# V's quads among the gate quads, and V's stores one to a product, in a hybrid decoder block on one Trainium2 core

## The chip, the cores and the metric

The kernel runs on one core of one Trainium2 chip. The core has five engines that run side by side: TensorE (PE: matmuls, with its weight loads listed as PEld), VectorE (DVE), ScalarE (ACT), GpSimd (POOL) and SyncE (SP), which here only issues DMAs. Each engine works through its own queue in order and waits on semaphores. The metric is the device time of one execution in microseconds (us). The kernel before the change takes 2109.99 us, the median of three runs (2107.88 to 2110.27).

## What is computed

One decoder block, for 2048 tokens of width 1024, all in float32. Cut to what matters here:

```python
proj = x @ w_in[l] + b_in[l]
q, k, v, g_attn, u_lru, g_lru, gate_logits = jnp.split(proj, SPLIT_POINTS, axis=-1)
q, k = rope(q), rope(k)                      # 3 groups of 8 heads of 64
for g, (window, dilation) in enumerate(((128, 1), (512, 4), (2048, 16))):
    o_g, lse_g = dilated_band_attention(q[:, :, g], k[:, :, g], v[:, :, g], window, dilation)
attn = sum over g of softmax(lse)_g * o_g
y_a = (attn * jax.nn.silu(g_attn)) @ w_attn_proj[l]
u = causal_depthwise_conv(u_lru, conv_w[l], conv_b[l])
y_b = (rg_lru(u, ...) * jax.nn.silu(g_lru)) @ w_lru_proj[l]
merged = sigmoid(gA) * y_a + sigmoid(gB) * y_b
x = layer_norm(ALPHA * x + merged @ w_out[l] + b_out[l])
```

The columns of proj form 72 tiles of 128: 12 each for q, k and v, 4 for the attention gate (ga), 8 each for u, its gate, and the two merge gates.

## The kernel before, in words

The kernel has three stages. The first, the projection, is the one that the change touches; it ends near 1454 us. Attention follows until about 1653 us, and then the merge and the output. Later stages read what the projection stored in device memory (names that end in _scr).

*The projection.* The 2048 tokens are worked in two halves of 1024. In each half the 72 column tiles go in 36 pairs, called quads here (two column tiles by two token chunks of 512), which gives 72 quads, numbered 0 to 71. Nearly all quads use Strassen's scheme in Winograd's form: 7 products in place of 8. There are 505 products in all. One product (function product, L602) is 12 matmuls of 128x128 by 128x512 (L620): over four row blocks, each of three terms, h times the input's high part, h times its low part, and l times the high part. h and l are the high and the low part of a weight block (fp32r), or of a sum of blocks (S). ACT makes h (L269), and l is made by DVE (L227, called at L275 in prep_w). In the first half the l's are also stored (wl_scr, L282); in the second they are loaded from there (L287).

*Order of the quads.* The table seq (L539 to L546) sets it: 2 merge-gate quads, then groups of "qk" quads (a k tile and a q tile) and "ug" quads (u and its gate), with places between them that take the next entry of the list light. In light stand first the six V quads, then two ga quads, then six merge-gate (mg) quads. So in each half the V quads stand at the places 4, 7, 9, 12, 15 and 17; ga at 20 and 23; mg at 25, 28, 31, 33 to 35. In the second half 36 is added to each.

*What follows a product.* The main loop (L941) goes through the products by number. For each it records the product's matmuls, then the steps that are due (weight loads load_w, L234; preparation of h and l three or four products ahead of their use), then run_chains (L187), then evacuate (L632), which adds the product into results. A finished result of 128x512 starts a chain, a generator that goes one step further when its Ask allows: a lag in products, a number of vacant slots, and a budget of time on the engines. The order in which this Python code records instructions is the order of every engine's queue.

- qk_chain (L299): four loads of a copy of the result with its 32-row blocks swapped (sw, L307, issued by SP), then at least two products later the rotation (y times cos, sw times sin, their sum, all at L227 on DVE, in the second half partly on POOL), then stores to k_scr, qh_scr and ql_scr.
- v_chain (L351): DVE transposes the result in 32x32 blocks (L355, vs<-y); then four stores to v_scr (L362), each 64 KB in pieces of 128 bytes, two after one product and two after the next at the earliest. A V quad has four results, so 16 stores; all twelve V quads have 192.
- mg_chain and silu_chain: the gates, on ACT mostly, with one store of 256 KB for each result.
- lru (L439): convolution and recurrence, on ACT and DVE.

*Slots.* Results, weights and helper tiles take 128x512 slots from one pool of NS = 32 (take, L133; the one that has been vacant longest comes first). give_sent (L150) gives a slot back two products after its last store was issued; whoever takes it next waits until that store has landed.

SP's queue therefore holds, in the order of the recording, weight loads, sw loads, stores of k, q, V, gates and l's, and in the second half the loads of l.

Of the kernel before, what the change touches and what calls it, by code (L numbers as in the profile page):

```python
# [26 lines left out]
FT_Q, FT_K, FT_V = 0, 12, 24  # L27
FT_GA, FT_U, FT_GL, FT_MA, FT_MB = 36, 40, 48, 56, 64
# [3 lines left out]
def hybrid_block_kernel(ctx: ExitStack, tc: tile.TileContext, a: dict, out: bass.AP):  # L32
    nc = tc.nc
    sp, act, dve, pool, pe = nc.sync, nc.scalar, nc.vector, nc.gpsimd, nc.tensor

    def flat(t):
        return t.bitcast(F32)
# [54 lines left out]
    late, pe_late = [], []  # L92

    def later(lag, fn):
        late.append((now["n"] + lag, fn))
# [4 lines left out]
    def run(queue):  # L100
        due = [x for x in queue if x[0] <= now["n"]]
        queue[:] = [x for x in queue if x[0] > now["n"]]
        for _, fn in due:
            fn()
# [19 lines left out]
    stA = ctx.enter_context(ExitStack())  # L124
    sl_p = stA.enter_context(tc.tile_pool(name="sl_p", bufs=1))
    ps = stA.enter_context(tc.tile_pool(name="ps", bufs=2, space=PSUM))
    NS, NL = 32, 4
    LATE = [7, 8, 9, 10, 11, 12, 13]
    TRACE = False
    vacant = list(range(NS))  # L130
# [2 lines left out]
    def take(name, dt=F32R):  # L133
        if not vacant:
            raise RuntimeError(f"no slot at {now['n']}: {[x[1].name if hasattr(x[1],'name') else x[1] for x in home.values()]} chains {len(chains)}")
        i = vacant[0]
        if name[0] == "y" and now["n"] >= base[NQ - 1]:
            i = next((x for x in LATE if x in vacant), i)
            if i in LATE:
                LATE.remove(i)  # L140
        vacant.remove(i)
        t = sl_p.tile([P, CH], dt, tag=f"s{i}", name=name)
        home[id(t)] = (i, t)
        return t

    def give(*ts):
        for t in ts:
            vacant.append(home.pop(id(t))[0])

    def give_sent(*ts):  # L150

        for t in ts:
            later(2, lambda t=t: give(t))
# [16 lines left out]
    chains = []  # L170
# [6 lines left out]
    def spend(**eng):  # L177
        for k, v in eng.items():
            if k == "DVE" and now["n"] < base[len(seq)] - 6:
                v *= ALONE  # L180
            left[k] = left.get(k, 0.0) - v
# [44 lines left out]
    def tt(eng, out, in0, in1, op):  # L226
        eng.tensor_tensor(out=out, in0=in0, in1=in1, op=op)  # L227
# [123 lines left out]
    def v_chain(vt, sgn, f, c):  # L351
        g, hp = divmod(f - FT_V, 4)
        yield Ask(need=1, DVE=.72)
        vs = take(f"vs{f}_{c}", F32)
        dve.transpose(vs, flat(vt))  # L355
        give(vt)
        dst = v_scr[g][hp // 2][c * CH:(c + 1) * CH].rearrange("(b i) f -> i b f", i=32)
        for a in range(4):
            if a % 2 == 0:
                yield Ask()  # L360
            f0 = (hp % 2) * P + 32 * a
            sp.dma_start(dst[:, :, f0:f0 + 32], vs[32 * a:32 * a + 32].rearrange("p (b f) -> p b f", f=32))  # L362
        give_sent(vs)


    def store_chain(t, dst):
        yield Ask()
        sp.dma_start(dst, t)
        give_sent(t)
# [49 lines left out]
    begun, gated, done = ({i: 0 for i in range(8)} for _ in range(3))  # L419
# [117 lines left out]

    qk = [("qk", FT_K + u, FT_Q + u) for u in range(12)]
    mg = [("mg", FT_MA + i, FT_MB + i) for i in range(8)]  # L539
    light = [("v", FT_V + 2 * j, FT_V + 2 * j + 1) for j in range(6)]  # L540
    light += [("ga", FT_GA + 2 * j, FT_GA + 2 * j + 1) for j in range(2)] + mg[2:]
    ug = [("ug", FT_GL + i, FT_U + i) for i in range(8)]
    seq = mg[:2]
    for i in range(8):
# [22 lines left out]
    def result(s, fi, c, bank, u):  # L567

        kind = plan[s][4]
        f = plan[s][1][fi][0]  # L570
        sgn = -1.0 if fi else 1.0
        nm = f"{f}_{c}"
        if u is None:
            y = take("y" + nm, F32)
            spend(ACT=.7)
            start_chain(mg_chain(y, 1.0, f, c, bank))
            return
        if kind in ("qk", "v"):
            y = take("y" + nm)
            total(flat(y), bank, u, f, sgn, True)  # L580
            start_chain(qk_chain(y, f, c) if kind == "qk" else v_chain(y, sgn, f, c))
        elif kind == "mg":
            y = take("y" + nm, F32)
            total(y, bank, u, f, sgn, False)
            start_chain(mg_chain(y, sgn, f, c))
        elif kind == "ga" or not fi:
            y = take("y" + nm, F32)
            total(y, bank, u, f, sgn, False)
            start_chain(silu_chain(y, sgn, f, c))
        else:  # L590
            i = f - FT_U
            if c == 1 and i in put_off:
                y = take("y" + nm, F32)
                total(y, bank, u, f, sgn, True)
                act.activation(ubs[:, i, 2, 0:3], y[:, CH - 3:CH], AF.Copy)
                start_chain(store_chain(y, u_scr[i]))
                return
            ub = ub_free.pop(0)
            total(ub[:, 3:3 + CH], bank, u, f, sgn, True)
            start_chain(lru(i, c, ub), 7 if c % 2 else 0)  # L600
# [31 lines left out]
    def evacuate(s, j):  # L632
        half, _, order, _, _ = plan[s]
        c0, c1 = 2 * half, 2 * half + 1
        if order is None:
            fi, k, c = PLAIN[j]
            if k:
                result(s, fi, c0 + c, Q["b"], None)
            return
        pid = order[j]  # L640
        b = Q[s, "p5"] if order is MID and pid in (5, 3) else Q["b"]
        if pid == 1:
            Q["e"] = take(f"e{s}", F32)
            act.activation(Q["e"], b, AF.Copy)
        elif pid == 2:
            result(s, 0, c0, b, Q["e"])
        elif pid == 6:
            Q["u2"] = take(f"u{s}", F32)
            tt(dve, Q["u2"], Q["e"], b, ALU.subtract)
        elif pid == 7:  # L650
            Q["u3"] = take(f"v{s}", F32)
            tt(dve, Q["u3"], Q["u2"], b, ALU.add)
        elif pid == 5:
            result(s, 1, c1, b, Q["u3"])
            if order is MID:
                Q[s, "u2"] = Q.pop("u2")
            else:
                tt(dve, Q["u2"], Q["u2"], b, ALU.add)
            if "p3" in Q:
                result(s, 0, c1, Q["p3"], Q["u2"])  # L660
                spend(DVE=.9)
        elif pid == 4:
            result(s, 1, c0, b, Q["u3"])
        elif order is MID:
            u2 = Q.pop((s, "u2"))
            result(s, 0, c1, b, u2)
            give(u2)
            return
        elif order.index(5) > j:
            Q["p3"] = take(f"p{s}", F32)  # L670
            act.activation(Q["p3"], b, AF.Copy)
        else:
            result(s, 0, c1, b, Q["u2"])
        last = {"e": (2, 6), "u2": (3, 5), "u3": (4, 5), "p3": (5,)}
        for n, p in last.items():
            if order is MID and n == "u2":
                continue
            if n in Q and pid in p and all(order.index(x) <= j for x in p):
                give(Q.pop(n))
# [119 lines left out]
    def unit(u):  # L799

        return (0, 2, 1)[u % 3], u // 3
# [139 lines left out]
    for T, (s, j) in enumerate(where):  # L941
        now["n"] = T
        for k in ("PE", "ACT", "DVE", "POOL"):
            left[k] = min(left[k], 0.0) + LEN
        if plan[s][2]:
            spend(**COST[plan[s][2][j]])
        product(s, j)
        for fn in events.pop(T, []):
            fn()
        run(late)  # L950
        run_chains()
        if T >= base[NQ - 1]:
            for fn in ((), first[:2], first[2:], (), second[:2], firstv, second[2:], ())[T - base[NQ - 1]]:
                fn()
        evacuate(s, j)
        low = min(low, len(vacant))
        if TRACE:
            print(T, s, j, plan[s][4], len(vacant), len(lo_vacant), len(chains), {k: round(v, 1) for k, v in left.items()})
    n = len(where)
    while chains or late or pe_late:  # L960
        now["n"] = n
        for k in left:
            left[k] = LEN
        run(pe_late)
        run(late)
        run_chains()
        n += 1
        assert n < len(where) + 60, (len(chains), late, pe_late)
# [171 lines left out]
    for i in range(NG):  # L1140
# [10 lines left out]
        light = copied and (unit((i - 2) // 4)[0] == 2 or i % 3 == 1 or i == 2)  # L1151
# [223 lines left out]
    for n in range(32):  # L1375
        c, f = divmod(n, 8)
# [159 lines left out]
    for tt in range(16):  # L1536
        c, b = divmod(tt, 4)
# [68 lines left out]
```

## Time and profile before

| | |
|---|---|
| median of 3 runs | 2109.99 us (2107.88 to 2110.27) |
| the profiled execution's own time | 2113.87 us |
| its span | 2112.2 us |
| PE busy | 2076.5 us (98%) |
| DVE busy | 1672.9 us (79%) |
| ACT busy | 1093.8 us (52%) |
| POOL busy | 472.0 us (22%) |
| SP's DMA queue | 480.63 MB in 349232 packets, 71.3% of 16 engines' span |
| V's stores | 192 of 64 KB, median 3.5 us from issue to landing |
| PE's share of the chain that ended last | 85%, L620 alone 58% |

A row of the profile names a line of the kernel, an engine, an operation and "out<-in" by the program's tile names, and then a count. In a timeline it begins with the start and the length in us, and brackets at its end hold the engine's idle time before it and what ended that. "SPq" is SP's queue at the time that it issues a DMA, which is not the time of the transfer. The profile comes from one execution, the times from others.

### The profile page before, as it was taken

The numbers are of one execution on the slowest core, as the hardware profiler recorded it, in microseconds if no ns is written. First come the engines' busy times: TensorE is split into PE (matmuls) and PEld (weight loads), VectorE is DVE, ScalarE is ACT, GpSimd is POOL, SyncE is SP. The second block draws the span as 40 slices with busy tenths as digits, with TensorE's granted clock in tenths as the row PEclk, the third lists the DMA queues.
The fourth block names the chain that finished last, engine by engine and source line by source line (L and its number), as shares of the span: only waits on it lengthen the run. The fifth ranks groups of instructions, "written<-read, shape, count | busy, mean of one in ns | idle before, by whom it ended". The sixth has DMA issues, their size and how long they took to land.

```text
span 2112.2 us, 35066 instructions
## 1 busy us (share of the span) xinstructions
PE 2076.5 (98%) x11696; PEld 1710.3 (81%) x11696; DVE 1672.9 (79%) x3146; ACT 1093.8 (52%) x2293; POOL 472.0 (22%) x436
## 2 busy tenths in 40 slices
PE   8999899999999999999998999999999999999998
PEld 7888788788888888887887888888888888888887
DVE  8889689788888878887886988976999645576667
ACT  6346246257356566556655775666999411211100
POOL 1111111111111012232221222221424344431120
PEclk9999999999999999999999999999999999999999
DMA  9898998988987967778788888779896798964432
GB/s 276 257 266 229 249 266 238 241 264 256 275 287 237 347 198 208 223 222 222 230 257 237 256 251 261 247 244 342 312 346 221 214 313 275 299 220 156 162 105 70
DMA packets 369590, 516.26 MB, mean 244 GB/s; under 512 B 173057, under 2 KB 178177, under 8 KB 366081
## 3 DMA queue, kind: packets, MB, share of 16 engines
q1 hardware_dynamic: 349232, 480.63, 71.3%
q0 software_dynamic: 12256, 19.42, 5.5%
q10 hardware_dynamic: 7920, 13.97, 1.9%
q8 instruction: 93, 1.52, 0.3%
q14 instruction: 89, 0.72, 0.1%
HBM read 312.95 MB, written 186.25 MB: 236 GB/s over the span
## 4 chain that ended last, share of the span: by engine, by line
PE 85%; ACT 5%; SPq 3%; DMA 3%; DVE 2%; issue 1%; DVEq 0%; ACTq 0%
PE q L620 58%; ACT p L1037 4%; PE yb L1354 3%; PE yb L1355 3%; PE z L1464 3%; PE z L1465 3%; PE yb L1356 3%; PE z L1466 3%; PE o L1078 2%; SPq L362 2%; PE s L1022 1%; PE ya L1432 1%; PE ya L1433 1%; PE ya L1434 1%; PE g L484 1%; PE pt L1048 1%
## 5 line engine op out<-in xcount | busy, mean ns | idle before, releaser
L620 PE MATMUL q<-xT,hS 128*128 128x512 f32 x1680 | 520.6, 391 | 0.0
L620 PE MATMUL q<-xT,l 128*128 128x512 f32 x1120 | 437.1, 390 | 4.0 <-DVE l L227 4.0
L620 PE MATMUL q<-xB,hA 128*128 128x512 f32 x1248 | 393.1, 396 | 11.9 <-ACT xB L215 5.6
L620 PEld LDWEIGHTS q<-xT,hS 128*128 128x128 f32 x1680 | 315.7, 189 | 70.6 <-issue 5.2
L620 PE MATMUL q<-xB,l 128*128 128x512 f32 x904 | 356.3, 394 | 9.0 <-DVE l L227 5.9
L620 PEld LDWEIGHTS q<-xB,hA 128*128 128x128 f32 x1248 | 237.0, 191 | 67.0 <-issue 6.7
L620 PEld LDWEIGHTS q<-xT,l 128*128 128x128 f32 x1120 | 211.1, 188 | 49.1 <-DVE l L227 4.9
L620 PEld LDWEIGHTS q<-xB,l 128*128 128x128 f32 x904 | 172.0, 190 | 47.6 <-DVE l L227 7.6
L269 ACT ACTIVATE hA<-wA 128x512 fp32r<-128x512 f32 x218 | 135.0, 622 | 92.5 <-DMA wA<-in_w_in_dram 26.3
L620 PE MATMUL q<-xT,hA 128*128 128x512 f32 x560 | 174.4, 393 | 0.0
L1037 ACT ACTIVATE p<-p,sta 128x256 f32<-128x256 f32 (+1 forms) x384 | 173.0, 473 | 1.1 <-DVE sta L1029 1.1
L245 POOL DMA_DIRECT2D wS<-in_w_in_dram x70 | 61.8, 955 | 497.7 <-DMA wS<-in_w_in_dram 158.0
L620 PE MATMUL q<-xB,hS 128*128 128x512 f32 x560 | 172.5, 389 | 0.0
L269 ACT ACTIVATE hS<-S 128x512 fp32r<-128x512 f32 x175 | 107.8, 622 | 97.1 <-DVE S L227 23.3
L227 POOL TENSOR_TENSOR S<-S,wA 128x512 f32<-128x512 f32 x35 | 48.7, 1392 | 425.0 <-DVE S L227 209.4
L227 DVE TENSOR_TENSOR y<-y,cos 128x512 f32<-128x512 f32 x96 | 81.1, 849 | 60.8 <-DMA sw<-y 60.6
L620 PEld LDWEIGHTS q<-xT,hA 128*128 128x128 f32 x560 | 105.2, 189 | 23.8 <-issue 2.2
L620 PEld LDWEIGHTS q<-xB,hS 128*128 128x128 f32 x560 | 105.0, 188 | 22.2 <-issue 0.4
L1029 DVE CUSTOM_DVE_ANT_0 p<-s,mask 128x256 f32<-128x256 f32 (+1 forms) x384 | 116.5, 360 | 0.2 <-PE s L1022 0.2
L1465 PE MATMUL z<-wo,mh 128*128 128x512 f32 (+1 forms) x264 | 101.0, 383 | 0.0
L1466 PE MATMUL z<-wo,ml 128*128 128x512 f32 (+1 forms) x264 | 101.0, 383 | 0.0
L1464 PE MATMUL z<-wo,mh 128*128 128x512 f32 (+1 forms) x264 | 101.0, 383 | 0.0
(204 smaller groups left out, 4165.3 us busy)
## 6 DMA issues: line engine op xcount, KB each, us to landing
wA<-in_w_in_dram SPq DMA_DIRECT2D x253, 256.0 KB, 4.7
wl_scr<-l SPq DMA_DIRECT2D x105, 512.0 KB, 4.9
l<-wl_scr SPq DMA_DIRECT2D x105, 512.0 KB, 4.4
sw<-y SPq DMA_DIRECT2D x384, 64.0 KB, 2.8
wS<-in_w_in_dram SPq DMA_DIRECT2D x70, 256.0 KB, 4.1
wS<-in_w_in_dram POOLq DMA_DIRECT2D x70, 256.0 KB, 6.4
v_scr<-vs SPq DMA_DIRECT2D x192, 64.0 KB, 3.5
B<-k_scr SPq DMA_DIRECT2D x24, 512.0 KB, 7.7
```

The source lines that it names most:

```text
L227: eng.tensor_tensor(out=out, in0=in0, in1=in1, op=op)
L245: pool.dma_start(t, w_part(s, x), accum_op=ALU.add)
L269: act.activation(h, r, AF.Copy)
L620: pe.matmul(bank, w[:, ks], x[:, kk, xx], start=(first and i == 0 and not onto), stop=(last and i == 11), skip_group_check=onto)
L1029: dve.tensor_tensor_reduce(out=st["p", i, j][:, h, lo:256], in0=st["s", i, j // 2][h][:, j % 2, lo:256], in1=mask[:, lo:256], scale=1.0, s ...
L1037: act.activation(p, p, AF.Exp, scale=-1.0, bias=s[:, h:h + 1], accum_out=s[:, 2 + h:3 + h])
L1354: pe.matmul(yb, WL[f][:, 0, k], xx[:, 0], start=(k == 0), stop=False)
L1355: pe.matmul(yb, WL[f][:, 0, k], xx[:, 1], start=False, stop=False)
L1356: pe.matmul(yb, WL[f][:, 1, k], xx[:, 0], start=False, stop=(k == 7))
L1464: pe.matmul(z, mh[:, k], w[:, 0, hs], start=(k == 0), stop=False)
L1465: pe.matmul(z, mh[:, k], w[:, 1, hs], start=False, stop=False)
L1466: pe.matmul(z, ml[:, k], w[:, 0, hs], start=False, stop=(k == 7))
```

## The change

Three edits, all in the projection. The list light now alternates V quads with ga and mg quads, so that V stands at the places 4, 9, 15, 20, 25 and 31 of each half, ga at 7 and 12, mg at 17, 23, 28 and 33 to 35; the qk and ug quads stay where they were. v_chain no longer issues its stores: it appends them to a list, v_store, and the main loop issues one at the end of each product's work, or two where the list holds more than six (and goes on after the last product until it is empty). The tile vs is given back after its fourth store, as before. NS is 34 in place of 32. Every engine has as many instructions as before, 192 V stores among them: before they were issued in groups of 2, 4, 6 or 8 after 55 of the products, now in groups of 1 or 2 after 148.

```diff
-    NS, NL = 32, 4
+    NS, NL = 34, 4
...
         vs = take(f"vs{f}_{c}", F32)
         dve.transpose(vs, flat(vt))
         give(vt)
+        yield Ask()
         dst = v_scr[g][hp // 2][c * CH:(c + 1) * CH].rearrange("(b i) f -> i b f", i=32)
         for a in range(4):
-            if a % 2 == 0:
-                yield Ask()
             f0 = (hp % 2) * P + 32 * a
-            sp.dma_start(dst[:, :, f0:f0 + 32], vs[32 * a:32 * a + 32].rearrange("p (b f) -> p b f", f=32))
-        give_sent(vs)
-
+            v_store.append((dst[:, :, f0:f0 + 32], vs[32 * a:32 * a + 32].rearrange("p (b f) -> p b f", f=32), vs if a == 3 else None))
+
+
+    v_store = []
+
+    def store_v():
+        for _ in range(1 + (len(v_store) > 6)):
+            if not v_store:
+                return
+            dst, part, done = v_store.pop(0)
+            sp.dma_start(dst, part)
+            if done is not None:
+                give_sent(done)
...
-    light = [("v", FT_V + 2 * j, FT_V + 2 * j + 1) for j in range(6)]
-    light += [("ga", FT_GA + 2 * j, FT_GA + 2 * j + 1) for j in range(2)] + mg[2:]
+    other = [("ga", FT_GA + 2 * j, FT_GA + 2 * j + 1) for j in range(2)] + mg[2:]
+    light = []
+    for j in range(6):
+        light += [("v", FT_V + 2 * j, FT_V + 2 * j + 1), other.pop(0)]
+    light += other
...
         evacuate(s, j)
+        store_v()
...
-    while chains or late or pe_late:
+    while chains or late or pe_late or v_store:
+        store_v()
```

Two places in SP's queue show what this moves. The first is where the V quad 9 of the first half has its stores, ahead of the sw loads of the qk quad 10. In the names, v_scr<-vs is a V store, sw<-y a load of a swapped copy, wA and wS are weight blocks and wl_scr<-l is a store of low halves. Before:

```order
L362 DMA v_scr_77<-vs_1_2302 32x16x32 x2
L362 DMA v_scr_77<-vs_0_2304 32x16x32 x2
L362 DMA v_scr_77<-vs_0_2332 32x16x32 x2
L362 DMA v_scr_77<-vs_1_2334 32x16x32 x2
L362 DMA v_scr_77<-vs_0_2332 32x16x32 x2
L362 DMA v_scr_77<-vs_1_2334 32x16x32 x2
L307 DMA sw_1_2395<-y_1_2368 32x512 x4
L234 DMA wA_12_2418<-in_w_in_dram 128x512
L282 DMA wl_scr_128<-l_11_2325 128x1024
L307 DMA sw_0_2423<-y_0_2400 32x512 x4
```

Four more V stores stand a little ahead of these twelve, with weight loads between, and a third row of sw loads follows after a weight load and a store. The same place after the change:

```order
L371 DMA v_scr_76<-vs_1_2298 32x16x32 x2
L307 DMA sw_1_2379<-y_1_2354 32x512 x4
L371 DMA v_scr_76<-vs_0_2300 32x16x32 x2
L234 DMA wA_12_2404<-in_w_in_dram 128x512
L282 DMA wl_scr_128<-l_11_2321 128x1024
L307 DMA sw_0_2409<-y_0_2384 32x512 x4
L371 DMA v_scr_76<-vs_0_2300 32x16x32 x2
L234 DMA wA_12_2435<-in_w_in_dram 128x512
L282 DMA wl_scr_127<-l_10_2373 128x512
L307 DMA sw_0_2442<-y_0_2414 32x512 x4
L371 DMA v_scr_76<-vs_0_2324 32x16x32 x2
```

With two stores a little ahead of these rows, four V stores now stand ahead of the first sw loads where sixteen stood, six ahead of the second and eight ahead of the third; the others follow behind.

The second place is the V quad 45 of the second half, ahead of the qk quad 46; l<-wl_scr is a load of low halves. SP's queue before:

```order
L362 DMA v_scr_77<-vs_3_9295 32x16x32 x2
L362 DMA v_scr_77<-vs_2_9297 32x16x32 x2
L362 DMA v_scr_77<-vs_2_9299 32x16x32 x2
L307 DMA sw_2_9341<-y_2_9306 32x512 x4
L287 DMA l_47_9363<-wl_scr_128 128x1024
L234 DMA wA_48_9365<-in_w_in_dram 128x512
L234 DMA wA_48_9367<-in_w_in_dram 128x512
L362 DMA v_scr_77<-vs_3_9295 32x16x32 x2
L362 DMA v_scr_77<-vs_2_9297 32x16x32 x2
L362 DMA v_scr_77<-vs_2_9299 32x16x32 x2
L362 DMA v_scr_77<-vs_3_9339 32x16x32 x2
L307 DMA sw_2_9385<-y_2_9346 32x512 x4
```

Two more weight loads, two V stores and the load l_48 follow these rows. After the change:

```order
L307 DMA sw_2_9331<-y_2_9302 32x512 x4
L371 DMA v_scr_76<-vs_3_9291 32x16x32 x2
L287 DMA l_47_9355<-wl_scr_128 128x1024
L234 DMA wA_48_9357<-in_w_in_dram 128x512
L234 DMA wA_48_9359<-in_w_in_dram 128x512
L307 DMA sw_2_9369<-y_2_9336 32x512 x4
L371 DMA v_scr_76<-vs_3_9291 32x16x32 x2
L234 DMA wA_48_9393<-in_w_in_dram 128x512
L234 DMA wA_48_9395<-in_w_in_dram 128x512
L371 DMA v_scr_76<-vs_2_9293 32x16x32 x4
L287 DMA l_48_9451<-wl_scr_129 128x1024
L307 DMA sw_3_9454<-y_3_9430 32x512 x4
```

Sixteen V stores stood ahead of the load l_48, and now eight do; the first sw loads of these rows, which stood behind six stores, stand ahead of all.

## The prediction

> **What bounds the kernel now.** I read the page first, then the busy time by stretches, the waits of TensorE (PE), and at each place where PE stood still the order of time on PE, VectorE (DVE) and SyncE's queue (SP). The page says that PE is nearly always busy:
>
> ```profile
> span 2112.2 us, 35066 instructions
> PE 2076.5 (98%) x11696; PEld 1710.3 (81%) x11696; DVE 1672.9 (79%) x3146; ACT 1093.8 (52%) x2293; POOL 472.0 (22%) x436
> ```
>
> So only PE's losses can be won. The projection ends near 1454 us; here are its stretches, for PE alone. Columns: from and to, length, PE busy (matmul records), granted clock, DMA share, GB/s.
>
> ```profile
> 30.00:230.00 200.00, 200.00 (x887) 1.00 0.90 255
> 230.00:260.00 30.00, 23.49 (x93) 0.89 0.86 229
> 260.00:400.00 140.00, 140.00 (x622) 1.00 0.91 252
> 400.00:430.00 30.00, 24.79 (x88) 0.83 0.87 250
> 430.00:955.00 525.00, 525.00 (x2331) 1.00 0.82 251
> 955.00:985.00 30.00, 28.20 (x117) 0.94 0.82 220
> 985.00:1120.00 135.00, 135.00 (x603) 1.00 0.82 238
> 1120.00:1150.00 30.00, 24.21 (x93) 0.83 0.79 214
> 1150.00:1440.00 290.00, 290.00 (x1291) 1.00 0.80 251
> 180.00:210.00 30.00, 30.00 (x134) 1.00 0.80 223
> ```
>
> PE is busy without a gap at clock 1.00, except in four stretches of 30 us; an undisturbed one (the last row) holds 134 matmuls. I call them stalls 1 to 4. The rows with which PE starts again (start, length, what, idle time before it and its releaser):
>
> ```profile
> 240.13 0.50 PE L620 MATMUL q<-xT,l 128*128 128x512 f32 x1 [1.90 <-DVE l L227]
> 244.22 0.70 PE L620 MATMUL q<-xB,hA 128*128 128x512 f32 x2 [1.53 <-DVE u L227]
> 247.99 0.79 PE L620 MATMUL q<-xB,l 128*128 128x512 f32 x1 [3.07 <-DVE l L227]
> 405.31 0.50 PE L620 MATMUL q<-xT,l 128*128 128x512 f32 x1 [2.13 <-DVE l L227]
> 409.67 0.70 PE L620 MATMUL q<-xB,hA 128*128 128x512 f32 x2 [0.21 <-DVE u L227]
> 413.24 0.79 PE L620 MATMUL q<-xB,l 128*128 128x512 f32 x1 [2.87 <-DVE l L227]
> 967.72 0.50 PE L620 MATMUL q<-xB,l 128*128 128x512 f32 x1 [1.80 <-DMA l<-wl_scr]
> 1131.62 1.22 PE L620 MATMUL q<-xB,hA 128*128 128x512 f32 x2 [4.56 <-ACT hA L269]
> 1134.08 0.79 PE L620 MATMUL q<-xB,l 128*128 128x512 f32 x1 [1.23 <-DMA l<-wl_scr]
> ```
>
> PE lacks weights: l (the low halves) that DVE has not made, or l and hA that come late by DMA. Behind this stands SP's queue; stall 1, then 2, on SP, with DVE's row between:
>
> ```profile
> 222.44 10.63 SPq L362 DMA_DIRECT2D v_scr<-vs  x12
> 233.17 2.41 SPq L307 DMA_DIRECT2D sw<-y  x4
> ...
> 237.20 0.69 DVE L227 TENSOR_TENSOR y<-y,cos 128x512 f32<-128x512 f32 x1 [12.49 <-DMA sw<-y]
> ...
> 388.15 10.18 SPq L362 DMA_DIRECT2D v_scr<-vs  x12
> ```
>
> Twelve V stores in one run hold SP for 10.63 us (0.89 each). The loads of a rotated copy (sw) stand behind them; DVE, which works in order, idles 12.49 us for sw, and its l's stand behind that wait. In the second half it is the weight loads that stand behind V's stores; stall 3:
>
> ```profile
> 943.12 4.01 SPq L362 DMA_DIRECT2D v_scr<-vs  x6
> 951.28 5.66 SPq L362 DMA_DIRECT2D v_scr<-vs  x8
> 960.86 0.96 SPq L362 DMA_DIRECT2D v_scr<-vs  x2
> 961.92 0.59 SPq L287 DMA_DIRECT2D l<-wl_scr  x1
> ```
>
> All four stalls lie where a V quad stands between two qk quads (sequence numbers 9, 17, 45 and 53).
>
> **What the stalls cost.** Against 134, the four stretches lack 41, 46, 17 and 41 matmuls, 145 in all; at 30/134 = 0.224 us that is 32.5 us. A second way: idle time is 120 - 100.7 = 19.3 us, and clock lost while busy is 23.49 x 0.11 + 24.79 x 0.17 + 28.20 x 0.06 + 24.21 x 0.17 = 12.6 us; together 31.9. I take the mean, 32.2 us. Even the shortest stall lowers the clock; the stretch behind its 1.80 us of idle time:
>
> ```profile
> 968.00:972.00 4.00, 4.00 (x13) 3.08 (x13) 3.97 (x6) 1.26 (x2) 1.89 (x2) 0.62 0.77 287
> ```
>
> So stall 3 costs 17 x 0.224 = 3.8 us, not 1.8. The Trainium skill (TensorE: Matmul & The Clock Gate, Part 1) says that the clock drops after an idle window of about 3.4 us; by that rule stall 3 would cost 1.8 us and the sum would be 30.2. The granted clock of 0.62 disagrees, and I go by it.
>
> **The change, part by part.** *Stores in a list.* Each of the 192 stores is still issued by SP, so nothing is removed; they move. At quad 9, 16 stores stood ahead of the first group of sw loads, and now 4 do; ahead of the third group 16, and now 8, two at the end of each of four products. At stall 1's price the first group comes 12 x 0.89 = 10.7 us earlier, the third 8 x 0.89 = 7.1. PE's idle time there was 1.90 by the first wait and 1.90 + 1.53 + 3.07 = 6.50 up to the third, so both are covered, the third by only 0.6 us. A store alone may be cheaper:
>
> ```profile
> L362 SPq DMA_DIRECT2D v_scr<-vs x192: 318/506/3482, 104.3 to 1127.6; - x192
> DMA to landing us min/median/max: 1.9/3.5/6.6
> ...
> 291.41 2.27 SPq L362 DMA_DIRECT2D v_scr<-vs  x2
> 293.79 3.55 SPq L307 DMA_DIRECT2D sw<-y  x4
> 270.00:300.00 30.00, 30.00 (x134) 24.84 (x133) 23.76 (x38) 14.73 (x23) 6.94 (x9) 1.00 0.92 233
> ```
>
> At the median of 0.506 us the eight that stay take 4.0 us and the cover is 3.7; at 1.14, as the pair at 291.41 that stood just ahead of sw loads, they take 9.1 against 14.2 before, and 6.5 - 5.1 = 1.4 us of stall would stay. I take the nearest, the run of stall 1: no stall. At stall 3's place (quad 45) the sixteen stores took 4.01 + 5.66 + 0.96 = 10.63 us ahead of the l load; eight now stand ahead, which is 5.3 us earlier against 1.80 of idle time.
>
> *The order of quads.* Places 17 and 53 hold a gate quad now, so stalls 2 and 4 lose all their V stores. V between two qk quads remains at 9 and 45 and is new at 25 and 61. At 25 six stores stand ahead of the third sw group, fewer than at 9; 61 resembles 45. Gate quads move up behind ug quads at 7, 12, 43 and 48. Before, a ga quad stood behind a ug quad at 20, 23, 56 and 59, and a gate quad between two qk quads at 25 and 61, all inside stretches without a gap (430 to 955, 1150 to 1440). Cost nothing; if ACT's longer silu chains collided at the early places, I bound it by one stall 3, 3.8 us.
>
> *Slots.* V's tile is held until its last store, up to about ten products longer. Before, slot reuse already cost a wait in stall 4:
>
> ```profile
> 1130.94 0.63 ACT L269 ACTIVATE hA<-wA 128x512 fp32r<-128x512 f32 x1 [11.37 <-DMA v_scr<-vs]
> ```
>
> Two more slots and a shorter queue work against that. Cost zero; at worst PE's 4.56 us behind this wait would come back once. The last V store now stands 16 products before the end of the projection (some 43 us at 12 x 0.224), and V's landing takes 3.5 us, so the attention stage waits for none. The slots' places in memory shift for it; its first rows show at most 0.97 us of PE idle time, which I leave, plus or minus 1:
>
> ```profile
> 1440.00:1470.00 30.00, 29.03 (x309) 24.41 (x309) 22.39 (x82) 19.58 (x65) 0.00 (x0) 1.00 1.04 398
> ```
>
> **The sum.** The profiled execution took 2113.87 us, 3.88 above the median of 2109.99. 2113.87 - 32.2 = 2081.7, less 3.88: **2077.8 us**, 32 us (1.5%) faster. What is late next is nothing of this size: PE would be busy from 30 to 1440 us.
>
> **The rivals.**
>
> *A rest of the stalls stays.* At 9 and 25 SP still runs late, with only 0.6 us of cover by the dearer price. For it: the pair at 1.14 us each. Against it: that pair stood in a stretch without loss (270 to 300). One place at stall 3's size gives 2081.6; one stall 1 (41 x 0.224 = 9.2) 2087. Chance 0.14.
>
> *The DMA engines, not SP's queue.* V's stores move 128-byte pieces, and the change keeps every piece. While the twelve stores ran, the engines were busy and moved little:
>
> ```profile
> 222.00:234.00 12.00, 12.00 (x55) 9.93 (x54) 2.70 (x5) 1.12 (x2) 3.88 (x6) 1.00 0.96 181
> ...
> 242.63 2.03 DMA sw<-y
> ```
>
> If their pieces delay the swaps, spreading them changes little: 2110, within 4 us. Against it: once issued, the sw load that ended stall 1 landed in 2.03 us; its lateness was spent ahead of its issue. The Trainium skill (DMA: Bandwidth & Descriptors, Issuing engines are not separate DMA queues) holds that the time a sequencer takes to issue a DMA is usually small beside the DMA; that speaks for this rival. The trace disagrees: 0.89 us of issue, twelve times, against a landing of 3.5. Chance 0.04.
>
> *Slower: stores among swaps.* Before, a quad's stores were over soon; now they trail through four groups of sw loads (three products in a row and one more), at each of twelve V quads. If a store behind swap loads cost SP more than 0.96 us (7.7 us of room over eight stores), place 9 would stall; if ten of the twelve stalled at stall 3's 3.8 us, the sum would turn. All twelve give 45.6: 2077.8 + 45.6 = 2123. For it: the longest store, 3.48 us. Against it: the median of 0.51, and that eight of the twelve V quads follow a ug quad, as eight did before without a stall (4, 7, 12, 15 and their like in the second half). Chance 0.04.
>
> **How the numbers follow.** The forecast has 0.75, with 2074 to 2082 for its own range (the 0.6 us between the two sums, the spread of runs of 2.4, and the start of the attention stage). 0.03 is left for something unnamed that still ends faster. Faster than 0.2% (4.2 us, about what a measurement can tell from no change): 0.75 + 0.14 + 0.03 = 0.92; within it 0.04; slower 0.04. The range reaches through the first rival: 2074 to 2088.
>
> **What would show it.** Right: V's stores on SP singly or in pairs with sw loads between them; DVE's longest wait for sw under 7 us, not 12.49; PE's waits for l and hA in the projection gone; clock 1.00 and some 134 matmuls in each 30 us from 30 to 1440; a span near 2080; and the same stages behind it. Wrong: a run of V stores of equal length still on SP, or sw loads that land late though issued early, or new PE waits at quads 9, 25, 45 or 61, or behind the gate quads at 7 and 12.

## The result and the profile after

| | before | after |
|---|---|---|
| median of 5 runs | 2110.27 us (2107.88 to 2112.91) | 2101.54 us (2100.95 to 2102.42) |
| ratio | | 0.9958, interval 0.9944 to 0.9973 |
| the profiled execution, its span | 2113.87, 2112.2 us | 2101.99, 2100.3 us |
| last matmul of the projection starts | 1453.54 us | 1441.63 us |

The change made the kernel 8.7 us (0.4%) faster. I had forecast 32 us and a range of 2074 to 2088; the direction was right, the size about a quarter of it. In the profiled executions 11.9 us were won, all of them in the projection: from its last matmul to the end of the span both kernels take 658.7 us.

The page of after:

```profile
span 2100.3 us, 35032 instructions
PE 2070.4 (99%) x11696; PEld 1706.2 (81%) x11696; DVE 1676.0 (80%) x3146; ACT 1093.1 (52%) x2293; POOL 474.9 (23%) x436
```

The busy time by stretches of after (from and to, length, PE busy and matmul records, granted clock, DMA share, GB/s):

```profile
30.00:230.00 200.00, 200.00 (x887) 1.00 0.90 261
230.00:260.00 30.00, 29.23 (x130) 1.00 0.92 240
390.00:420.00 30.00, 29.03 (x129) 1.00 0.93 263
420.00:540.00 120.00, 119.99 (x531) 1.00 0.88 261
540.00:570.00 30.00, 28.29 (x124) 1.00 0.86 207
570.00:600.00 30.00, 25.52 (x101) 0.89 0.99 303
600.00:1260.00 660.00, 660.00 (x2932) 1.00 0.81 245
1260.00:1290.00 30.00, 28.49 (x124) 1.00 0.90 237
1290.00:1320.00 30.00, 27.99 (x119) 0.94 0.78 242
1320.00:1440.00 120.00, 120.00 (x533) 1.00 0.83 256
```

Stalls 1 to 4 of before are not there in their form: the stretch from 600 to 1260 us, in which stalls 3 and 4 lay, has no gap and clock 1.00. But from 540 to 600 and from 1260 to 1320 us, where before had none, matmuls are missing now. The rows with which PE starts again in after:

```profile
261.86 0.50 PE L493 MATMUL g<-vl,gw 64*128 64x512 f32 x2 [2.64 <-DVE vl L227]
401.12 0.50 PE L632 MATMUL q<-xB,l 128*128 128x512 f32 x1 [0.97 <-DVE l L227]
558.62 0.50 PE L632 MATMUL q<-xB,l 128*128 128x512 f32 x1 [1.20 <-DVE l L227]
567.13 0.70 PE L632 MATMUL q<-xT,hS 128*128 128x512 f32 x2 [0.51 <-DVE y L227]
578.93 0.51 PE L493 MATMUL g<-vh,gw 64*128 64x512 f32 x2 [2.00 <-ACT vh L483]
581.91 0.79 PE L493 MATMUL g<-vl,gw 64*128 64x512 f32 x2 [2.48 <-DVE vl L227]
1277.44 0.50 PE L632 MATMUL q<-xB,l 128*128 128x512 f32 x1 [0.45 <-DMA l<-wl_scr]
1284.25 0.50 PE L632 MATMUL q<-xB,l 128*128 128x512 f32 x1 [1.07 <-DMA l<-wl_scr]
1300.16 0.50 PE L632 MATMUL q<-xB,l 128*128 128x512 f32 x1 [2.01 <-DMA l<-wl_scr]
```

I give such a stall's cost as its loss: the time from each matmul's start to the next, less 0.2267 us for each product matmul between (the pace of undisturbed stretches) and 0.15 for each gate matmul, so that idle time and lost clock are both in it. A stall belongs to the V quad behind which it lies. By place, in us:

| V at place | 9 | 17 | 25 | 45 | 53 | 61 | sum |
|---|---|---|---|---|---|---|---|
| before | 9.1 | 10.4 | 0 | 3.7 | 9.3 | 0 | 32.4 |
| after | 2.8 | 1.1 | 9.8 | 0 | 0 | 5.4 | 19.2 |

How far a stall is followed changes such a loss by up to 1 us. At 17 and 53 after has no V quad; the 1.1 is the wait at 401.12, for an l. The sums differ by 13.2 against 11.9 in the spans; the rest is spread in pieces too small to sort. Of 32 us forecast, about 15 came back at places 25 and 61.

**What is late at place 25.** First SP's queue in after, while V's stores of place 25 trail through the products behind it; the last three rows are ACT's and DVE's:

```profile
545.99 2.73 SPq L307 DMA_DIRECT2D sw<-y  x4
548.76 1.15 SPq L371 DMA_DIRECT2D v_scr<-vs  x2
...
551.12 2.63 SPq L307 DMA_DIRECT2D sw<-y  x4
553.81 1.14 SPq L371 DMA_DIRECT2D v_scr<-vs  x2
...
560.44 3.08 SPq L307 DMA_DIRECT2D sw<-y  x4
563.57 0.58 SPq L371 DMA_DIRECT2D v_scr<-vs  x1
...
566.91 3.02 SPq L377 DMA_DIRECT2D u_scr<-y  x1
569.98 1.61 SPq L371 DMA_DIRECT2D v_scr<-vs  x1
571.64 0.67 SPq L234 DMA_DIRECT2D wA<-in_w_in_dram  x1
...
572.83 0.44 SPq L371 DMA_DIRECT2D v_scr<-vs  x1
573.31 1.26 SPq L234 DMA_DIRECT2D wA<-in_w_in_dram  x1
577.73 0.63 ACT L269 ACTIVATE hA<-wA 128x512 fp32r<-128x512 f32 x1 [5.13 <-DMA wA<-in_w_in_dram]
578.26 0.61 ACT L483 ACTIVATE vh<-v 128x512 fp32r<-128x512 f32 x1
577.72 0.69 DVE L227 TENSOR_TENSOR S<-wS,wA 128x512 f32<-128x512 f32 x1 [2.60 <-DMA wA<-in_w_in_dram]
```

V's stores now stand singly and in pairs among the sw loads, as the change says. Follow the last rows: the weight load (wA) recorded with product 195 is issued at 571.64 us, and the next one at 573.31. The first is for the qk quad 29. ACT, in order, idles 5.13 us for it, and vh stands behind it at 578.26; vh is what PE waits for at 578.93 (the gate matmuls of the ug quad before), and vl, DVE's part of the same, comes later still. PE's queue stands for these gates, and then the clock falls to 0.89.

How late SP runs can be measured: the start of an issue, less the start on PE of the product with which it was recorded (found by counting matmuls, 12 to a product; L620 has 6072 of them in the profile of before, which makes 506 products, not the 505 named above). Product 195 starts at 554.1 in after, so its weight load is 571.64 - 554.1 = 17.5 us late; before, where a merge-gate quad stood at place 25, it was 8.0. That is the backlog. From the start of its issue to its landing the load took 6.0 us in after and 4.2 before, so that most of what it came later by is the queue's. At place 9 the third sw group was 21.3 us late before and is 12.0 in after, 9.3 us where I had worked out 7.1. Not all of that is the list's: with 34 slots and V's stores as before (slots_alone below) it is 16.8. The sum of SP's issue times in the projection hardly changed: 860 us before, 857 after.

Two more views answer to those of before: DVE's waits for sw, in all, times, longest (before: 60.6, 20, 12.5); and V's stores by their line:

```profile
DVE y L227 <- DMA sw<-y: 38.3, 20, 3.7
```

```profile
L371 SPq DMA_DIRECT2D v_scr<-vs x192: 318/547/1849, 104.2 to 1398.5; - x192
DMA to landing us min/median/max: 2.0/3.9/7.8
```

The long wait for sw is gone, and V's stores land in 3.9 us. At place 61 the same backlog shows by what the second half loads: PE waits for l itself, by DMA (the last three restart rows), and ACT waits 6.48 us for a slot whose V store is late. The l loads recorded with products 445 and 447 are 7.3 and 8.7 us late in after, against 2.3 and 1.7 before.

```profile
1273.52 0.64 ACT L269 ACTIVATE hA<-wA 128x512 fp32r<-128x512 f32 x1 [6.48 <-DMA v_scr<-vs]
```

### The profile page after: what moved, and what is told of

The parts are those of the page before. It is cut to its first block, busy times and chain, and to the rows that moved or that the text cites. A ratio compares the mean times of both kernels' runs of the same rounds, so it can differ in the third digit from the quotient of the medians.

```text
span 2100.3 us, 35032 instructions
## 1 busy us (share of the span) xinstructions
PE 2070.4 (99%) x11696; PEld 1706.2 (81%) x11696; DVE 1676.0 (80%) x3146; ACT 1093.1 (52%) x2293; POOL 474.9 (23%) x436
```

## The experiments

Three theories stood. **A**: it is SP's queue, which runs late wherever V's sixteen stores stand between two qk quads; the change moved that from 17 and 53 to 25 and 61. **B**: the DMA engines are full, V's 128-byte pieces above all; SP is only held up by them. **C**: the gate quads that moved up cause the new waits. All kernels were timed in five rounds against the kernel before.

### The parts of the change

*The order and the slots, with V's stores as before*, two after one product and two after the next. From after, cut to what matters:

```diff
-            v_store.append((dst[...], vs[...], vs if a == 3 else None))
+            sp.dma_start(dst[...], vs[...])
...
-        store_v()
```

> The changed order of quads and 34 slots, with V's stores issued as before, in bursts out of v_chain. Theory A (backlog on SP's queue: what counts is how much SP has to issue where a V quad stands between two qk quads; now at 9, 25, 45 and 61): four stalls again, two of about 9 us in the first half (9 and 25) and two of 4 to 9 in the second (45 and 61), 2100 to 2115 us. Theory B (the DMA engines, kept busy by the 128-byte pieces): the same count of stalls, so the same time; this run doesn't tell A from B. Theory C (the gate quads at their new places cost DVE and ACT time, with or without the list): the new waits of the changed kernel are all here, at the gates (vh, vl) behind places 9 and 25, on top of the stalls: over 2115.

2105.57 us (2104.77 to 2108.65), ratio 0.9978 (0.9970 to 0.9987). Losses: 6.4 at place 9, 9.5 at 25, 2.0 at 45, 9.1 at 61, none at 17 and 53. PE's waits in this kernel (in all, times, longest):

```profile
PE q L623 <- DMA l<-wl_scr: 7.6, 2, 5.7
PE q L623 <- DVE l L227: 5.6, 2, 3.0
```

They are the kinds of before, l by DVE and l by DMA, at the places where V now stands. The stalls went with V.

*The list and the slots, with the quads in their old order.*

```diff
...
-    light = []
-    for j in range(6):
-        light += [("v", ...), other.pop(0)]
-    light += other
+    light = [("v", ...) for j in range(6)]
+    light += [("ga", ...) for j in range(2)] + mg[2:]
```

> The list and 34 slots, with the quads in the order of before, so V stands between qk quads at 9, 17, 45 and 53, close behind other V quads. Theory A: each of the four stalls shrinks to a tail of the size that the changed kernel shows at 25 (8 to 10 us) or at 9 (3 us), since the stores that move off the first sw loads fall on the weight loads behind: 2088 to 2102. Theory B: the engines have the same pieces at the same places, stalls hardly smaller: 2100 to 2110. Theory C (gate quads): none of the new waits, 2078 to 2085.

2095.26 us (2090.99 to 2099.65), 0.9929 (0.9916 to 0.9942). Losses: 6.1 at place 9, about 7 at 17, about 3 at 53. With no gate quad moved, its main waits are still these:

```profile
PE g L493 <- DVE vl L227: 7.2, 2, 4.3
```

So gate matmuls wait although the gate quads stand where they stood: against C. And this is faster than the whole change: with the list, the new order costs rather than gains.

*The slots alone*: before, with one number changed.

```diff
-    NS, NL = 32, 4
+    NS, NL = 34, 4
```

> The kernel before with 34 slots in place of 32 and nothing else. If slots matter (chains go on earlier with more vacant ones, and V's bursts are shorter, and less reuse waits for V's stores in the second half): stalls 3 and 4 shrink, 2100 to 2107. Theory A without slots: 2107 to 2113, as before.

2103.3 us (2101.42 to 2104.02), 0.9965 (0.9953 to 0.9978): 7 us for two slots. The stalls stay at all four places, each smaller (4.3, 6.9, 1.7 and 8.7). Before, ACT waited three times for a slot whose V store had not landed, 18.9 us in all; here it has no such wait. That is one thing that the slots change; whether it is all of the 7 us isn't shown.

### Where V stands

*V behind ug quads only, with the list.* V at 4, 7, 12, 15, 20 and 23, so none between two qk quads; gate quads stand there instead.

```diff
+    vq = [("v", ...) for j in range(6)]
...
+    light = [(vq if i in (0, 1, 3, 4, 6, 7) else other).pop(0) for i in range(14)]
```

> The changed kernel with its six V quads of a half at 4, 7, 12, 15, 20 and 23, all behind a ug quad and none between two qk quads; gate quads at the rest (9, 17, 25, 28 and so on). Theory A: SP's queue has no V store at the four tight places, so nearly all of the remaining 20 us goes: 2080 to 2086. Theory B: the same pieces at other places where the engines are as busy (DMA share 0.8 to 1.0 all through): 2090 to 2102. Theory C: gate quads between qk quads do as much harm as V: 2095 to 2105.

2083.9 us (2083.25 to 2084.79), 0.9875 (0.9861 to 0.9890). Losses 2.4 in all. For A, and against C: gate quads stand between qk quads at 9, 17 and 25 here and lose 0, 0.4 and 2.0, and nothing in the second half; at 25 V's stores of place 23 were spread just ahead.

*The same places with V's old stores*, and 34 slots, made from before.

```diff
-    NS, NL = 32, 4
+    NS, NL = 34, 4
...
+    light = [(vq if i in (0, 1, 3, 4, 6, 7) else other).pop(0) for i in range(14)]
```

> V quads at 4, 7, 12, 15, 20 and 23 of each half, as in the run with the list there, but V's stores in bursts out of v_chain as before the change, and 34 slots. Theory A, with place as the first cause: before the change V at 4, 7, 12 and 15 lost nothing with bursts, so place alone brings nearly all: 2080 to 2088, and the list adds nothing there. Rival (the list is what helps, the place only a little): 2095 to 2105.

2081.38 us (2081.19 to 2081.65), 0.9864 (0.9850 to 0.9877): the fastest of all, without the list. The busy time of PE from 30 us to just before the projection's end is one row without a gap:

```profile
30.00:1418.00 1388.00, 1388.00 (x6160) 1.00 0.85 256
```

The list isn't needed there. With it (the run ahead) the median is 2.5 us higher, but that comparison is across two chips, and the two ratios' intervals overlap.

*The same with 32 slots*: before, with nothing but light changed.

```diff
...
+    light = [(vq if i in (0, 1, 3, 4, 6, 7) else other).pop(0) for i in range(14)]
```

> The kernel before with only the places of V changed: 4, 7, 12, 15, 20 and 23 of each half, bursts as before, 32 slots as before. Place alone (theory A): PE loses nothing at the four old places, 2080 to 2086, since with 34 slots it was 2081.4. If the two slots were needed there too (alone they brought 7 us): 2086 to 2092.

2088.01 us (2087.00 to 2088.66), 0.9895 (0.9881 to 0.9908). V's places alone give 22 us, two slots 6.6 more on top (again across chips). Its profile still loses some 7 us, most of it in waits for l of 0.82, 2.88 and 1.08 us near 242, 402 and 1171 us, which old_at_ug doesn't have.

*The change, with only place 25 (and so 61) undone*: V at 28 instead, a merge-gate quad at 25.

```diff
...
+    light = [(vq if i in (0, 2, 4, 6, 9, 10) else other).pop(0) for i in range(14)]
```

> The changed kernel with one V quad of each half moved from 25 (between two qk quads) to 28 (behind a ug quad); list and 34 slots stay. Theory A, priced by the changed kernel's profile: the 9.8 us lost behind place 25 and the 5.4 behind 61 go, 4 us at 9 and 17 stay: 2086 to 2089. Rival (SP's work is only moved on, and turns up behind 28 and 64): 2098 to 2103.

2087.64 us (2087.38 to 2088.84), 0.9894 (0.9881 to 0.9908): 14 us better than the whole change. SP's queue at place 25, to be laid beside that of after:

```profile
556.38 2.42 SPq L307 DMA_DIRECT2D sw<-y  x4
561.17 2.49 SPq L377 DMA_DIRECT2D u_scr<-y  x1
563.72 0.42 SPq L234 DMA_DIRECT2D wA<-in_w_in_dram  x1
564.74 0.38 SPq L234 DMA_DIRECT2D wA<-in_w_in_dram  x1
```

Without V's stores the first wA goes out at 563.72 us, for a product that starts at 557.0: 6.7 us late, not 17.5. The losses at 25 and 61 are gone; from 290 us on PE has next to no gap, and no stall came up behind 28 and 64 instead. What is left lies at place 9, some 8 us:

```profile
260.00:290.00 30.00, 26.29 (x107) 0.89 0.76 247
290.00:1440.00 1150.00, 1149.25 (x5215) 1.00 0.85 256
```

*Three V quads of each half between qk quads*: 34 slots, V's old stores, V at 4, 9, 17, 20, 25 and 31, made from before. This is the test in the other direction.

```diff
-    NS, NL = 32, 4
+    NS, NL = 34, 4
...
+    light = [(vq if i in (0, 2, 5, 6, 8, 10) else other).pop(0) for i in range(14)]
```

> Bursts and 34 slots, with V at 4, 9, 17, 20, 25 and 31 of each half: three V quads of a half between two qk quads in place of two. Theory A: each such place costs what the runs with bursts and 34 slots showed there: about 4 to 6 at 9, 7 at 17, 9.5 at 25, 2 at 45, 9 at 53 and 9 at 61, 41 to 43 us on the 2081.4 of the run without such places: 2119 to 2126, slower than before the change. Rival (the count of such places is not it; it is how close V quads follow each other, and these are spread wide): 2095 to 2108.

2117.12 us (2114.13 to 2119.48), 1.0033 (1.0023 to 1.0042): slower than before in spite of two more slots, and just under the 2119 to 2126 that A gave. Losses at 9, 17, 25, 45, 53 and 61: 3.8, 7.1, 5.5, 3.8, 2.4 and 9.4. All six places stall, and by the waits that before had:

```profile
PE q L621 <- DVE l L227: 10.6, 4, 3.0
PE q L621 <- DMA l<-wl_scr: 9.3, 3, 5.1
```

### SP's queue or the DMA engines

*V's stores issued by ACT.* From after; the bytes and pieces stay, SP is rid of 192 issues.

```diff
-            sp.dma_start(dst, part)
+            act.dma_start(dst, part)
```

> The changed kernel with V's 192 stores issued by ACT and not by SP, at the same places in the order. The pieces and the engines that move them stay; SP's queue loses some 119 us of issue time and ACT gains as much. Theory A: SP's lateness at 25 falls from 15 to 17 us to about 10, the waits of the gates and of l go: 2080 to 2088, unless ACT's own queue is pushed past its slack (then the waits are for hA and vh made by ACT, up to 2100). Theory B: sw and weight loads are issued earlier but land as late, PE's waits stay: 2096 to 2104. Theory C: no change: 2099 to 2104.

2091.53 us (2090.57 to 2091.91), 0.9910 (0.9898 to 0.9923): 10 us better than after, between the two theories. Losses 1.7 at place 9, 4.2 at 17, 1.8 at 25, about 2 at 61. The stores now take 87 us of issue time from ACT's queue, so this edit is not free on the other side. The Trainium skill (DMA: Bandwidth & Descriptors, Issuing engines are not separate DMA queues), which the prediction weighed, holds issue time to be usually small beside the DMA. By it this edit should have moved little; the 10 us disagree.

*V's stores in wide pieces*: 32 pieces of 2 KB for each store in place of 128-byte ones, which fill v_scr in another order; SP issues them as in after. Attention then works on V in a wrong order, with the same instructions and sizes, so this kernel and the next are good for their time alone.

```diff
-            v_store.append((dst[:, :, f0:f0 + 32], vs[32 * a:32 * a + 32].rearrange(...), ...))
+            r0 = 64 * (16 * (hp % 2) + 4 * c + a)
+            v_store.append((v_scr[g][hp // 2][r0:r0 + 64].rearrange("(p x) f -> p (x f)", x=2), vs[32 * a:32 * a + 32], ...))
```

> The changed kernel with V's 192 stores still of 64 KB each and at the same places in SP's queue, but each written in 32 pieces of 2 KB in place of 512 of 128 bytes. V then lies in another order in memory, so attention works on V in a wrong order, with the same instructions and sizes. Theory A (SP's queue is late by the time that it takes to issue): what counts is the length of a store's issue on SP; if it stays near 0.6 us the waits stay, 2098 to 2103, and if it falls to 0.3 to 0.4 us (as the shortest stores and weight loads show) some half of them goes, 2088 to 2096. Theory B (the engines, full of small pieces, hold up every DMA): all of it goes, issues of sw and of u_scr shorten too, 2080 to 2086.

2090.75 us (2088.50 to 2093.27), 0.9911 (0.9897 to 0.9925): 11 us better than after, where A had allowed 2088 to 2096 for shorter issues and B 2080 to 2086. Losses 0.6 at 9, 3.8 at 25, 3.8 at 61. But wide pieces are also issued faster (547 ns median in after, 432 here), so this edit eases the queue as well and doesn't part the two by itself:

```profile
L371 SPq DMA_DIRECT2D v_scr<-vs x192: 302/432/1997, 102.0 to 1385.8; - x192
```

*Both at once*: wide_pieces with ACT's issue.

```diff
-            sp.dma_start(dst, part)
+            act.dma_start(dst, part)
```

> The changed kernel with both: V's stores issued by ACT, and in pieces of 2 KB (V in another order in memory, so attention works on V in a wrong order, with the same instructions and sizes). Alone, the queue brought 10 us and the pieces 11, of some 20. If the queue and the pieces are two separate causes: both gains, 2079 to 2083. If they are one (either alone takes what there is to take, and what stays with ACT is ACT's own delay): 2088 to 2092.

2083.9 us (2081.33 to 2085.15), 0.9880 (0.9864 to 0.9897). Each edit won 10 to 11 us, both together 17.6 (16.6 by the gains over before on each chip): more than either, less than the sum of 21. That lies outside both expectations, nearer to two causes than to one. No stall is left in its profile, which is the fastest of its four executions: there V between qk quads costs nothing, with SP rid of the stores and the pieces wide. The row of the same stretch as above, for this kernel:

```profile
30.00:1418.00 1388.00, 1388.00 (x6160) 1.00 0.82 256
```

The same bytes in the same time take 0.82 of the engines where V's narrow pieces took 0.85. B has a part, then: the queue is what runs late, and the narrow pieces are some of why. SP's issue times in the projection suggest how. Those of V's stores add up to 115 us in after and 103 in wide_pieces; those of SP's other 1288 DMAs to 742 and 711. With ACT issuing V, these others take 736 us with narrow pieces and 713 with wide ones (721 to 762 in the other kernels, all with narrow pieces).

*The stores held back until SP is calm*: a counter of SP's DMAs (0.85 us each against 2.72 us for a product) lets the list go on only when it stands near zero, or when slots run short.

```diff
+        queue["late"] = max(0.0, queue["late"] + 0.85 * queue["n"] - 2.72)
+        for _ in range(2):
+            if not v_store or queue["late"] > 0.5 and len(vacant) > 3:
+                return
```

> The changed kernel and its order of quads, but a V store is issued only after products with few other DMAs on SP (a running count of 0.85 us a DMA against 2.72 a product has to be near zero), or when at most three slots are vacant. At 9 and 25 the stores then come behind the next weight loads; at 61 the slots run short and they come two to a product as before. Theory A: the waits of the first half (14 of some 19 us) go, those at 61 stay: 2086 to 2092. Theory B: pieces only move, 2096 to 2103. Theory C: the gate quads' waits stay, 2099 to 2104.

2099.75 us (2098.87 to 2101.70), 0.9952 (0.9940 to 0.9965): it missed. The projection did end earlier, its last matmul at 1427.7 us and so 14 us ahead of after's, with losses of some 7 in all. But the stores ran on past the projection's end: seven of them were issued from 1433.30 us on, and attention had to wait. The chain of waits at that turn, and DVE's and PE's rows:

```profile
1429.57 7.29 DMA mg_scr<-y
1436.88 6.89 DMA v_scr<-vs
...
1443.93 0.42 DVE L1054 CUSTOM_DVE_ANT_0 p<-s,mask 128x256 f32<-128x256 f32 x1 [11.70 <-DMA v_scr<-vs]
1444.42 1.99 PE L1047 MATMUL s<-B,A 64*128 64x256 f32 x12 [10.19 <-DVE sta L1054]
```

Two stores that follow one another, 14.2 us in all, end what DVE waits 11.70 us for, and PE 10.19 behind it. DVE reads nothing of V there; by the kernel's text its tile p takes over memory of the projection's slots, from which the store still had to read. What was held back in the first stage was paid for at the door of the second.

## Why the prediction was wrong

**Stores in a list: right for the sw loads, not for the stall at 9.** At place 9 the sw groups came earlier than forecast (9.3 us for the third, not 7.1, some of it by the slots), DVE's longest wait fell to 3.7 us, and the stall for l and u is gone. The 2.8 us that stay lie further on, at the gates of the next ug quad, and list_alone and v_28_for_25 lose 6.1 and some 8 there, where the kernels with 34 slots and the old stores lose 3.8 to 6.4. With 34 slots in both, the list took the losses of the second half from 10.4 to about 3 us in the old order (slots_alone, list_alone) and from 11.1 to 5.4 in the new (order_alone, after), but those of the first from 11.2 to about 13 and from 15.9 to 13.7: no clear gain. At 45 the loss is zero, as said.

**Places 17 and 53: right.** Without V they lose 1.1 and 0 in after.

**Places 25 and 61: the step that failed.** It said: "At 25 six stores stand ahead of the third sw group, fewer than at 9; 61 resembles 45." That counted the stores ahead of the sw loads alone. All sixteen are new at this place, and a queue that works in order doesn't lose the ten that stand behind the sw loads: eight of them and the longer u_scr store stand ahead of the first weight load of the qk quad 29, which came 17.5 us late instead of 8.0. From there hA, vh, vl and l were late, and PE with them: 9.8 and 5.4 us. v_28_for_25 shows it, since V's removal from that place alone takes both losses away. The same omission made "What is late next is nothing of this size" wrong. I had asked what is late for those stalls that I knew, and not for the places to which V was moved.

**Slots: mis-sized.** Zero was forecast; alone they are worth 7 us on before, and 6.6 with V behind ug quads. The row of before that showed a wait of 11.37 us for a slot was a hint that I set at zero.

**Gate quads: right.** Zero was forecast, and list_at_ug, with gate quads at more places, has 2.4 us of loss in all.

**The start of attention: right**, within what a row shows; the time behind the projection is the same 658.7 us.

**The sum's subtraction of 3.88 us was wrong too.** A kernel without any stall in the projection exists: old_at_ug, at 2081.38 us, where I had 2077.8. Its profiled execution took 2081.26, so the price of the four stalls was right (2113.87 - 32.2 = 2081.7). But the 3.88 by which before's profiled execution stood above its median could not be taken off once more: before's five runs spread over 5.0 us, old_at_ug's four over 0.5. The spread may lie in the stalls and go with them, but that isn't shown: wide_on_act has no stall in its profile, and its four executions spread over 3.8 us.

**The rivals.** "A rest of the stalls stays" came nearest, as it named place 25, but it held one place at 3.8 or 9.2 us and not 19.2 over four. "The DMA engines, not SP's queue" is not what happened, but has a part (wide_pieces, wide_on_act). The slower case did not come, though three_between_qk shows that it was near: with V at three such places in each half and no list, the kernel is slower than before.

**What the parts come to.** Slots alone -7.1 us; with the order -5.5; slots with the list -15.8; all three -8.7 (each against before on its own chip). The order that the change brings costs 1.6 us with the old stores and 7.1 with the list. The order that pays is another, V behind ug quads.

**What stays open.** How much of the narrow pieces' cost comes from their own longer issue (547 against 432 ns) and how much from other DMAs held up by full engines was not parted by a run; the sums of issue times above point more to the others (31 and 23 us of queue time against 12), without showing what lengthens an issue. Why the losses at 9, 53 and 61 differ from kernel to kernel by several us with V at the same place isn't explained either. It need not be the kernel: after and v_28_for_25 record the same instructions up to product 179, and in their profiles place 9 loses 2.8 and some 8 us. So a loss at one place of one profile can be off by 5 us, and the times of all executions decide, not the single losses.

## What to carry to other kernels

A queue that is worked in order keeps its work: when something is moved in it, list what stands behind it at the new place, up to the point where the queue has caught up, not only what stood behind it at the old one. Measure first how late the queue runs at each place (the start of an issue against the work with which it was recorded): here, choosing places where it had room gave 22 us without any new code, and moving V to two other places without room gave back half of what the change had won, spread or not: place 25 lost 9.8 us with the list and 9.5 without it. Work that is held back to a quiet time also needs an end: look at what the next stage waits for first.

## What the runs showed of the hardware

- The issue of one store from SP varies far more than I had allowed: the 256 KB store u_scr took 3.02 us in after and 2.49 in v_28_for_25 at the same place, and a V store 0.32 to 1.85 us.
- Two waits of 2.00 and 2.48 us, with matmuls between them, cost 7.8 us in all: the granted clock fell to 0.89 over the 30 us that hold them (570 to 600), as it had behind stall 3's 1.80 us.
- Two more slots of 128x512 for a pool of 32 were worth 7 us of 2110, although PE was busy 98% of the time.
